# Attention's projections moved ahead of the delta rule's scan and the state space projections

## The chip, the core and the metric

The kernel runs on one core of a Trainium2 chip. The metric is device time in microseconds (us) of one execution; lower is better. The core has a matrix engine (PE, with its weight loads shown apart as PEld), a vector engine (DVE), a scalar engine (ACT), a general engine (POOL) and a queue (SP) that here issues most of the data transfers. Each engine runs its own instructions in a fixed order and waits where an input or a buffer is not ready.

## The reference

One layer of a hybrid encoder on x of 1024 tokens by 1024 channels, in float32. One normalised input feeds three mixers through one combined projection:

```python
h = rmsnorm(x, pre_mix_norm)
proj = h @ w_in        # columns: a_q, a_k, a_v | s_z, s_xbc, s_dt | g_qkv, g_z, g_b, g_a
att = swa_sink_alibi(a_q, a_k, a_v, sinks)      # 4 heads of 64, 2 key heads; keys of this and the 2 chunks before
ssd = ssd_mixer(s_z, s_xbc, s_dt, ...)          # causal conv of 4 taps, SiLU, chunked scan, gate, norm
gdn = gdn_mixer(g_qkv, g_z, g_b, g_a, ...)      # conv, SiLU, per chunk a triangular solve, then a scan
x = x + rmsnorm(concat[att, ssd, gdn] @ w_out, post_mix_norm)
h = rmsnorm(x, pre_ffn_norm)
x = x + rmsnorm((silu(h @ w_gate) * (h @ w_up)) @ w_down, post_ffn_norm)
```

Chunks are 64 tokens; the scans of ssd and gdn carry a state from chunk to chunk.

## The kernel before

**Two halves, then the feed-forward part.** Tokens are treated in two halves of 512, each in four tiles of 128 (t = 0 to 3). `half(h, hT, order)` runs the mixers of a half; `hT` is its normalised, transposed input, kept as a high and a low part so that each product is three matmuls (`gemm`, `gemm_rows`). Then comes the feed-forward block for all tokens, which the change does not touch.

**The steps of a half** are letters in a string of `ORD`, one string a half:

- K (`keys`): `decay_block` (the gate gz, decays), four convolved projections for keys and queries, for each tile `gdn_pre` (matmul `gram`, products `Wn`, `QK`), and at last `gdn_diag`: the diagonal blocks of all tiles are sent through memory (`cd`, `Wst`) and solved in 31 dependent steps on DVE, each a product `Tpr` and a sum `Tst`.
- V (`values`): two convolved projections gv.
- G0 to G3 (`scan`): with G0 and G2 the rest of the inverse (`gdn_inv`, matmuls lx, lv, lX, lV), then the scan of a tile.
- S0, S1 (`ssd_blocks`): per group four convolved projections (B, C, x0, x1) and the gate z. s00 to s13 (`ssd`): state space tile of group g and tile t; DVE scales the matrix `sE`, PE multiplies it in `y`.
- A (`att_blocks`): four projections without a convolution: two of queries (aq, whose weights are loaded as two halves of 64 columns), ak, av. a0 to a3 (`att`): two `att_tile` each, with PE's as, tp_p and ao.
- N (`after`): loads and normalises the next half's input into new `hT` tiles; they take the place of the old ones once the last projection of this half has read those.
- O (`block_first`, in the second half's string): the output projection, residual and norms of the first half; its `mT` also takes the place of `hT`.

**A convolved projection** (`conv_block`) is 24 matmuls, two splits of weights (high part on ACT, low part alternately on POOL and DVE), and on DVE three taps of 128x512 (line 348) and a last step (line 352); ACT copies, scales and takes a tanh. A gate projection (z) has 96 smaller matmuls, and per tile one tanh and one step of 128x256 on DVE (line 362). A projection of A has 24 matmuls, the splits, and one ACT copy.

**What sets the order.** The program is handed to a planner. The order of the text, and with it the order of the letters, is each instruction's priority; the planner fills every engine's queue with the first instruction by priority that by its own estimate is ready and has its buffer. Loads of weights have a raised priority. The order that comes out is fixed, and the engines keep to it. So a step that stands later in the string can still be placed earlier, as filler, where PE would otherwise stand still.

**Buffers that matter.** The pool tag "act" has `ACTS = 16` tiles of 128x512: a half takes 2 for gz, 2 for gv, 6 for each of S0 and S1 (B, C, x0, x1, two z), 4 for A; ak and av live on until a0 of the next half. Projections share two PSUM banks (`ps_mm`), raw weights three buffers, split weights six pairs.

The order of steps is read here:

```python
steps = dict(O=lambda: o0.append(block_first()), K=keys, V=values, G=scan, S=ssd_blocks, s=ssd, A=att_blocks, a=att, N=after)
for step in order.split():
    steps[step[0]](*[int(c) for c in step[1:]])
```

Of the kernel before, what the change touches and what calls it, by code (L numbers as in the profile page):

```python
# [28 lines left out]
KQS = 2  # L29
SB = 2  # L30
WC = 544
ORD = ("K V G0 G1 G2 G3 S0 s00 s01 s02 s03 S1 s10 s11 s12 s13 A N a0 a1 a2 a3",
       "K V G0 G1 G2 G3 S0 s00 s01 s02 s03 S1 s10 s11 s12 s13 A a0 a1 O a2 a3")
STEPS = (1, 1, 2)
EARLY = (2, 4)
LEAD, SLEAD = 260, 90
# [35 lines left out]
def trunk(ctx, tc, a):  # L72
# [855 lines left out]
    load_rest()  # L928
    hT = half(0, hT, ORD[0])
    half(1, hT, ORD[1])  # L930
    mT_h0 = o0[0]
# [388 lines left out]
```

## Time and profile before

| | |
|---|---|
| median of 3 runs | 1284.45 us (1283.5 to 1286.0) |
| profiled execution | 1280.08 us; span from first to last instruction 1278.3 us |
| PE busy | 1223.0 us, 96% of the span |
| DVE busy | 946.3 us, 74% |
| ACT busy | 574.6 us, 45% |
| POOL busy | 224.4 us, 18% |
| mean granted TensorE clock | 0.986 of full speed |
| data moved | 168.57 MB, mean 132 GB/s |

Busy time of an engine is the union of its instructions. "Idle before" an instruction is time its engine stood still just ahead of it, and the name behind the arrow is what released it. In a table by stretch the columns are busy us of each engine (or of the one chosen tile or line) with instruction counts in brackets, then the granted TensorE clock, the share of the transfer engines' time, and GB/s. L348 is line 348 of the kernel. The mixers of the first half lie at about 30 to 290 us, those of the second at about 235 to 550, overlapping.

### The profile page before, as it was taken

The numbers are of one execution on the slowest core, as the hardware profiler recorded it, in microseconds if no ns is written. First come the engines' busy times: TensorE is split into PE (matmuls) and PEld (weight loads), VectorE is DVE, ScalarE is ACT, GpSimd is POOL, SyncE is SP. The second block draws the span as 40 slices with busy tenths as digits, with TensorE's granted clock in tenths as the row PEclk, the third lists the DMA queues.
The fourth block names the chain that finished last, engine by engine and source line by source line (L and its number), as shares of the span: only waits on it lengthen the run. The fifth ranks groups of instructions, "written<-read, shape, count | busy, mean of one in ns | idle before, by whom it ended". The sixth has DMA issues, their size and how long they took to land.

```text
span 1278.3 us, 19099 instructions
## 1 busy us (share of the span) xinstructions
PE 1223.0 (96%) x6624; PEld 1017.1 (80%) x6624; DVE 946.3 (74%) x1890; ACT 574.6 (45%) x1261; POOL 224.4 (18%) x313
## 2 busy tenths in 40 slices
PE   5999999999998999978999999999999999999997
PEld 4878788887787889867987888888888887888885
DVE  5687996787799485653478998886676756768885
ACT  7454444455434353553456434333333334443661
POOL 3243455224344532100010000000000000000000
PEclk9999989999999999889999999999999999999999
DMA  7322332133332322366244465543333268676315
GB/s 238 83 72 78 87 82 74 48 104 91 97 79 57 94 96 67 108 211 219 92 162 165 148 221 164 168 142 97 124 102 113 97 231 287 185 229 214 94 57 197
DMA packets 161413, 168.57 MB, mean 132 GB/s; under 512 B 29567, under 2 KB 117915, under 8 KB 161317
## 3 DMA queue, kind: packets, MB, share of 16 engines
q1 hardware_dynamic: 143892, 133.53, 34.8%
q10 hardware_dynamic: 17424, 33.82, 7.0%
q8 instruction: 52, 0.85, 0.3%
q14 instruction: 45, 0.36, 0.1%
HBM read 127.21 MB, written 40.11 MB: 131 GB/s over the span
## 4 chain that ended last, share of the span: by engine, by line
PE 82%; DVE 9%; DMA 4%; ACT 2%; issue 1%; POOL 1%; SPq 0%; ACTq 0%; POOLq 0%; DVEq 0%
PE mm_p L1187 5%; PE mm_p L1188 5%; PE mm_p L1189 5%; PE mm_o L206 2%; PE mm_o L208 2%; PE mm_o L207 2%; DVE Tpr L513 1%; PE gram L487 1%; DMA yb<-in_ffn_w_down_dram 1%; PE y L676 1%; PE ao L755 1%; PE as L719 1%; PE mm_z L206 1%; PE mm_z L207 1%; PE mm_z L208 1%
## 5 line engine op out<-in xcount | busy, mean ns | idle before, releaser
L169 POOL TENSOR_TENSOR rsq<-ssv,mhalf 128x1 f32<-128x1 f32 x32 | 20.7, 655 | 752.2 <-DVE ssv L259 743.2
L513 DVE TENSOR_TENSOR Tpr<-Tst,Wst 128x32 f32<-128x32 f32 (+30 forms) x62 | 48.5, 782 | 4.4 <-POOL Wst L508 3.7
L206 PE MATMUL mm_o<-wh_wo,hhi_m 128*128 128x256 f32 x128 | 36.8, 287 | 1.1 <-DVE hlo_m L236 1.1
L206 PE MATMUL mm_z<-wh_z,hhi_a 128*128 128x256 f32 x128 | 37.7, 295 | 0.0
L208 PE MATMUL mm_z<-wh_z,hlo_a 128*128 128x256 f32 x128 | 36.6, 286 | 0.0
L207 PE MATMUL mm_z<-wl_z,hhi_a 128*128 128x256 f32 x128 | 36.5, 285 | 0.0
L208 PE MATMUL mm_o<-wh_wo,hlo_m 128*128 128x256 f32 x128 | 36.1, 282 | 0.0
L207 PE MATMUL mm_o<-wl_wo,hhi_m 128*128 128x256 f32 x128 | 36.0, 282 | 0.0
L676 PE MATMUL y<-xs,sE 128*128 128x64 f32 x128 | 19.9, 285 | 7.8 <-DVE sE L669 7.8
L1070 DVE TENSOR_TENSOR o<-mm_o,pm_row 128x256 f32<-128x256 f32 x16 | 6.8, 424 | 27.9 <-PE mm_o L208 27.9
L515 DVE TENSOR_REDUCE Tst<-Tpr 128x16 f32<-128x32 f32 (+30 forms) x62 | 26.7, 431 | 0.6
L676 PEld LDWEIGHTS y<-xs,sE 128*128 128x128 f32 x128 | 18.5, 203 | 9.7 <-DVE sE L669 8.4
L185 ACT ACTIVATE wh_wo<-wr_wo 128x512 fp32r<-128x512 f32 x24 | 15.1, 630 | 24.7 <-DMA es<-e00s 5.0
L206 PEld LDWEIGHTS mm_o<-wh_wo,hhi_m 128*128 128x128 f32 x128 | 24.1, 188 | 2.5 <-issue 1.9
L213 PE MATMUL mm_x<-hlo_a,wh_x 128*128 128x512 f32 x64 | 25.8, 403 | 0.0
L212 PE MATMUL mm_x<-hhi_a,wh_x 128*128 128x512 f32 x64 | 25.6, 400 | 0.0
L214 PE MATMUL mm_x<-hhi_a,wl_x 128*128 128x512 f32 x64 | 25.5, 398 | 0.0
L206 PEld LDWEIGHTS mm_z<-wh_z,hhi_a 128*128 128x128 f32 x128 | 24.8, 194 | 0.5
L207 PEld LDWEIGHTS mm_z<-wl_z,hhi_a 128*128 128x128 f32 x128 | 24.6, 192 | 0.3
L208 PEld LDWEIGHTS mm_z<-wh_z,hlo_a 128*128 128x128 f32 x128 | 24.7, 193 | 0.0
L208 PEld LDWEIGHTS mm_o<-wh_wo,hlo_m 128*128 128x128 f32 x128 | 24.1, 188 | 0.3 <-issue 0.3
L207 PEld LDWEIGHTS mm_o<-wl_wo,hhi_m 128*128 128x128 f32 x128 | 24.1, 188 | 0.0
(1683 smaller groups left out, 4481.4 us busy)
## 6 DMA issues: line engine op xcount, KB each, us to landing
wr_wo<-in_w_out_dram SPq DMA_DIRECT2D x32, 256.0 KB
x<-in_x_dram SPq DMA_DIRECT2D x8, 512.0 KB
wr_x<-in_w_in_dram SPq DMA_DIRECT2D x16, 256.0 KB
wr_z<-in_w_in_dram SPq DMA_DIRECT2D x16, 256.0 KB
res<-in_x_dram SPq DMA_DIRECT2D x8, 512.0 KB
resf<-x1d SPq DMA_DIRECT2D x8, 512.0 KB
mixn<-mixd SPq DMA_DIRECT2D x12, 256.0 KB
wr_e<-in_ffn_w_gate_dram SPq DMA_DIRECT2D x12, 256.0 KB
```

What stands on the lines that cost most here:

```text
L206: pe.matmul(ps, hi[:, tsl], whi, start=k == 0, stop=False)
L207: pe.matmul(ps, hi[:, tsl], wlo, start=False, stop=False)
L208: pe.matmul(ps, lo[:, tsl], whi, start=False, stop=k == len(wp) - 1)
L212: pe.matmul(ps, whi, hi, start=k == 0, stop=False)
L213: pe.matmul(ps, whi, lo, start=False, stop=False)
L214: pe.matmul(ps, wlo, hi, start=False, stop=k == len(wp) - 1)
L513: vec.tensor_tensor(pr[:, :, 0:i + 1], T[:, :, 0:i + 1], W[:, None, 0:i + 1, i].to_broadcast([P, CW, i + 1]), op=ALU.mult)
L515: vec.tensor_reduce(T[:, :, i], pr[:, :, 0:i + 1], axis=AX, op=ALU.add)
L676: pe.matmul(yd[:, j], E[:, j, :], xs[:, j], start=True, stop=True)
L1187: pe.matmul(ps[j], ah[:, s], bh, start=i == 0, stop=False)
L1188: pe.matmul(ps[j], ah[:, s], bl, start=False, stop=False)
L1189: pe.matmul(ps[j], al[:, s], bh, start=False, stop=i == NP - 1)
```

## The change

The letter A, four projections, moves in both strings from behind the last state space tile to the place right behind V. Nothing is added or removed; the instructions of A get a higher priority than those of G, S and s.

```diff
-ORD = ("K V G0 G1 G2 G3 S0 s00 s01 s02 s03 S1 s10 s11 s12 s13 A N a0 a1 a2 a3",
-       "K V G0 G1 G2 G3 S0 s00 s01 s02 s03 S1 s10 s11 s12 s13 A a0 a1 O a2 a3")
+ORD = ("K V A G0 G1 G2 G3 S0 s00 s01 s02 s03 S1 s10 s11 s12 s13 N a0 a1 a2 a3",
+       "K V A G0 G1 G2 G3 S0 s00 s01 s02 s03 S1 s10 s11 s12 s13 a0 a1 O a2 a3")
```

## The prediction

> **What bounds the kernel now.** I read the busy times by stage first, because the change moves work inside the first 640 us only. Columns: stretch, length, busy us of PE, PEld, DVE, ACT, POOL with instruction counts, granted TensorE clock, DMA share, GB/s.
>
> ```profile
> 64.00:115.00 51.00, 51.00 (x224) 37.10 (x223) 37.71 (x76) 27.41 (x59) 23.04 (x40) 1.00 0.31 84
> 115.00:187.00 72.00, 67.73 (x405) 59.02 (x404) 71.23 (x137) 29.23 (x71) 33.25 (x37) 0.95 0.27 72
> 347.00:416.00 69.00, 64.23 (x394) 56.15 (x393) 68.25 (x134) 31.74 (x76) 31.45 (x31) 0.98 0.27 71
> 528.00:576.00 48.00, 36.98 (x200) 31.51 (x200) 27.00 (x74) 25.19 (x65) 4.38 (x8) 0.82 0.60 189
> ```
>
> PE is the limit nearly everywhere. It falls short in one stretch of each half, where DVE is the limit (71.23 of 72 us, 68.25 of 69): PE idles 4.27 and 4.77 us there. The third hole is the end of the first half's output block, 11.02 us idle in 528 to 576. Total PE work does not change, so the result is what happens to these three holes.
>
> What fills DVE there is the delta rule's diagonal solve (the lines Tpr, Tst of gdn_diag): 31 dependent steps a half. First the timeline of DVE with the first and last step of each half, then the groups by line (busy us, mean ns, idle before).
>
> ```profile
> 115.05 0.20 DVE L513 TENSOR_TENSOR Tpr<-Tst,Wst 128x32 f32<-128x32 f32 x1 [2.48 <-POOL Wst L508]
> 186.61 0.67 DVE L515 TENSOR_REDUCE Tst<-Tpr 128x16 f32<-128x512 f32 x1
> 344.98 1.27 DVE L513 TENSOR_TENSOR Tpr<-Tst,Wst 128x32 f32<-128x32 f32 x1 [1.23 <-POOL Wst L508]
> 414.50 0.68 DVE L515 TENSOR_REDUCE Tst<-Tpr 128x16 f32<-128x512 f32 x1
> ...
> L513 DVE TENSOR_TENSOR Tpr<-Tst,Wst 128x32 f32<-128x32 f32 (+30 forms) x62 | 48.5, 782 | 4.4 <-POOL Wst L508 3.7
> L515 DVE TENSOR_REDUCE Tst<-Tpr 128x16 f32<-128x32 f32 (+30 forms) x62 | 26.7, 431 | 0.6
> ```
>
> So (48.5 + 26.7) / 2 = 37.6 us of a 72 us stretch are the solve, and the convolved projections and state space tiles beside it take the rest. The PE timeline and the list of PE's waits show how that reaches PE, which runs in its written order: it stands at a state space tile's matmul until DVE has scaled sE.
>
> ```profile
> 162.49 0.69 PE L676 MATMUL y<-xs,sE 128*128 128x64 f32 x2 [3.96 <-DVE sE L669]
> 396.03 0.74 PE L676 MATMUL y<-xs,sE 128*128 128x64 f32 x4 [3.60 <-DVE sE L669]
> ...
> PE y L676 <- DVE sE L669: 7.8, 3, 4.0
> PE tp_f L230 <- ACT o L878: 5.5, 2, 3.7
> ```
>
> **The change, part by part.** *Moved matmuls.* A is four projections of 24 matmuls a half. One costs 47.50 - 41.94 = 5.56 us, by the first matmuls of two neighbours in the PE timeline; four make 22.2 us. In before they run, interleaved, from 179.13 to 214.98, right after the solve.
>
> ```profile
> 41.94 0.40 PE L212 MATMUL mm_gk<-hhi_a,wh_gk 128*128 128x512 f32 x1
> 47.50 0.40 PE L212 MATMUL mm_gq<-hhi_a,wh_gq 128*128 128x512 f32 x1
> ...
> 179.13 0.58 PE L212 MATMUL mm_aq<-hhi_a,wh_aq 128*128 128x512 f32 x1
> 214.98 0.40 PE L214 MATMUL mm_av<-hhi_a,wl_av 128*128 128x512 f32 x1
> ```
>
> Where they go is seen from the stretch 80 to 115 by tile: S0's B, then its two x.
>
> ```profile
> 80.00:115.00 35.00, 6.49 (x24) 1.00 0.32 88
> 80.00:115.00 35.00, 11.60 (x48) 1.00 0.32 88
> ```
>
> V has ended by 80, and S0's four convolved blocks (B, C at 6.5 each, x 11.6: 24.6) fill the stretch with 35 - 24.6 = 10.4 us of other matmuls, mostly K's small ones. With A in their place it is 80 + 22.2 + 10.4, so A ends near 113, about where the solve begins. PE was full there and stays full: cost 0 by itself. The same holds for half 1, where the solve's first step is 230 us later.
>
> *What stands beside the solve.* Pushed back by 22 us, S0's four convolved blocks now start near 113 instead of 80. PE's share of the stretch by tile, first z, then aq, then x, B, C (the last three add up to 24.8 in the stretch):
>
> ```profile
> 115.00:187.00 72.00, 25.62 (x191) 0.95 0.27 72
> 115.00:187.00 72.00, 6.88 (x27) 0.95 0.27 72
> 115.00:187.00 72.00, 12.18 (x48) 0.95 0.27 72
> 115.00:187.00 72.00, 6.34 (x24) 0.95 0.27 72
> 115.00:187.00 72.00, 6.26 (x24) 0.95 0.27 72
> ```
>
> z is light for DVE, a convolved block heavy. DVE's share, first the three taps (L348), then the last step (L352), then the group means of the z gate and of aq's split:
>
> ```profile
> 115.00:187.00 72.00, 13.76 (x15) 0.95 0.27 72
> 115.00:187.00 72.00, 4.08 (x6) 0.95 0.27 72
> ...
> L362 DVE SCALAR_TENSOR_TENSOR z<-gth_z,mm_z 128x256 f32<-128x256 f32 x16 | 6.6, 410 | 0.0
> L186 DVE TENSOR_TENSOR wl_aq<-wr_aq,wh_aq 128x512 fp32r<-128x512 f32 x4 | 4.3, 1081 | 0.0
> ```
>
> Out of the stretch go the second z (half of 25.62 = 12.8 us of PE), aq (6.9) and both x of S1 (12.2), 31.9 in all. In come S0's four blocks (24.8 by the same rows) and, to fill up, the first x of S1 (6.1): PE -1.0. DVE goes from five blocks (15 taps) to seven: +2 x (13.76 + 4.08) / 5 = +7.1; four z gates fewer, -4 x 0.41 = -1.6; two aq splits fewer, -2 x 1.08 = -2.2. DVE +3.3. Where DVE sets the length, PE's idle grows by 3.3 + 1.0 = 4.3 us a half.
>
> *The head start.* Before 115, DVE gets A's splits (the cheapest split row is 0.69; four, 2.8) in place of about three blocks (3 x 3.57 = 10.7): 7.9 us of DVE are free while gdn_pre makes the solve's input. If all of that shortened the road to the solve, it would start 7.9 us earlier beside light work; if PE's order sets that road, 0. The row says DVE already waited there for ACT, and DVE idled 51 - 37.71 = 13.3 us of that stretch, so I take nearer the low end, 2.3 us. Net +2.0 a half, **+4.0** for both; bounds -3.6 x 2 and +4.3 x 2.
>
> ```profile
> 99.87 0.69 DVE L471 TENSOR_REDUCE ssq<-sq 128x8 f32<-128x512 f32 x1 [1.94 <-ACT sq L466]
> ```
>
> *Buffers.* The pool "act" has 16 tiles. In before gz 2, gv 2, S0 6 and S1 6 fill it exactly, and A waits until S0's are free. Now A holds 4 until the last attention tile, and S1 finds two; its other x and z wait until S0's tiles are through, as A did. In half 1 the previous ak and av hold two more until a0. Their matmuls can run ahead into the two ps_mm banks; behind the evacuation that waits on ACT stand the next splits. Between nothing (today's wait for the same release hides) and a stall of one tile's round a half (the larger gap above, 3.96, twice, = 8), I take 0, since state space and attention tiles are ready for PE meanwhile.
>
> *DMA queue.* aq's weights come as halves. A issues 12 loads a half, against 8 for four convolved projections, so 4 more stand on SP in front of S0's loads and of the solve's own stores and loads.
>
> ```profile
> 147.42 12.42 SPq L184 DMA_DIRECT2D wr_aq<-in_w_in_dram  x8
> ...
> L184 SPq DMA_DIRECT2D wr_aq<-in_w_in_dram x16: 368/432/1009, 147.4 to 392.6; - x16
> ```
>
> 4 x 0.43 = 1.7 us of issue. The loads are covered by the three raw buffers and a full PE; without that cover, or if the solve's loads are what comes late, it is 1.7 us of later solve a half. I take 0 of 0 to 1.7.
>
> *The tiles a0 to a3* become ready 100 us earlier and are the planner's filler for PE's gaps. What is spent there is missing later: in 528 to 552 their tiles as, tp_p and ao keep PE busy beside the normalisation chain of O.
>
> ```profile
> 528.00:552.00 24.00, 3.20 (x8) 0.79 0.33 108
> 528.00:552.00 24.00, 2.83 (x12) 0.79 0.33 108
> 528.00:552.00 24.00, 4.07 (x24) 0.79 0.33 108
> ...
> L726 DVE SCALAR_TENSOR_TENSOR asc<-cst,as 128x256 f32<-128x256 f32 (+1 forms) x32 | 11.6, 398 | 6.7 <-PE as L719 6.7
> L729 DVE TENSOR_REDUCE am<-asc 128x2 f32<-128x512 f32 (+1 forms) x16 | 10.4, 648 | 0.2
> ```
>
> PE 10.1 us for about three of the 16 attention tiles, 3.4 each; DVE 22.0 / 16 = 1.4 each in these two rows alone, with six smaller operations behind, so as filler beside the solve they bring no large gain. Done before 528, they leave up to 10.1 us more idle (+10.1); left where they are, 0. a2 and a3 still stand behind O, so I take **+1.5**, about half a tile.
>
> *Clock.* The stretches after the 3.96 us gap show what a gap costs beyond itself: 8 x 0.31 + 8 x 0.12 = 3.4 us of clock at most. I count no new gap, 0 of 0 to 3.4 a half.
>
> ```profile
> 158.00:166.00 8.00, 4.04 (x19) 3.67 (x18) 8.00 (x14) 2.30 (x4) 3.65 (x5) 0.69 0.28 68
> 166.00:174.00 8.00, 8.00 (x58) 7.50 (x57) 8.00 (x17) 2.75 (x9) 2.93 (x3) 0.88 0.12 33
> ```
>
> The Trainium skill, "TensorE: Matmul & The Clock Gate", section "What's actually happening", says that an idle window of about 3.4 us halves the array's clock until it was busy about as long; the trace agrees (gap 3.96 us, clock 0.69 then 0.88). By it, 4.3 us added as one new gap in each half would cost an estimated 1.7 us more each, and the sum would be +8.9 in place of +5.5.
>
> **Sum:** +4.0 + 1.5 = +5.5 us. The profiled execution took 1280.08 us (span 1278.3), 4.4 below the median of the three runs, 1284.45; on that median I get **1290**.
>
> **Rivals.** *Faster, by the head start:* if the solve starts 4.3 us earlier than today (before 111 and 341 us), the stretch breaks even; from there on each us closes the holes, at most 4.27 + 4.77, so 1284.45 - 9 = 1275.4. For it: 13.3 us of idle DVE ahead of the solve. Against: PE's dense order sets where gdn_pre's gram matmuls come. *Faster, at the end:* attention's rows of half 1 are stored earlier, the second output block's transposes move up and fill the 11.02 us hole; with most of it, -8, 1276. Against: that hole's own chain waits for o (5.5 us on ACT alone), and the loads share a queue. *No change:* filler replaces filler, holes trade places, 1284.5. For it: PE's total is the same and 96% busy. *Clearly slower, by buffers:* S1 stalls for S0's tiles in both halves, 8 us, on top of the +5.5: 1298. *The change does nothing,* because the planner issues by readiness: part of no change, unlikely since A is ready as soon as V is.
>
> **How the numbers follow.** 0.2% is 2.6 us, about what a measurement of this kernel can tell from no change. Chances: forecast 0.33 (1287.1 to 1294), buffers 0.12, no change 0.23, head start 0.20, end 0.12. So slower 0.45, same 0.23, faster 0.32. Range: the fast cases reach to 1275.4, the buffer case to 1298 with 3.4 of clock on top; leaving out a tenth at each end gives 1277 to 1301; the forecast's own is 1287 to 1294.
>
> **What the profile after would show.** Right: aq's matmuls near 80 and 310 us; the solve starting 2 us earlier and taking longer; PE's waits for sE above 7.8 us; S1's second z after the solve; fewer attention matmuls after 528 us. Wrong: PE idle under 4 us in both stretches, or the solve ending before 180 us; or the hole after 528 filled by tp_m.

## The result, and the profile after

The changed kernel takes 1300.77 us, the median of four runs (1297.55 to 1305.57), against 1284.03 (1283.5 to 1286.0) for the kernel before in the same session. The ratio is 1.0131, with a 95% interval of 1.009 to 1.0171: slower by 16.7 us. The forecast was 1290 with a range to 1301, so the sign is right and the measured change is three times the forecast one.

The profiled execution took 1297.55 us (span 1295.7, mean granted clock 0.973; before 1278.3 and 0.986). PE's busy time rose from 1223.0 to 1235.0 us and its idle time from 55.3 to 60.7. The work is the same, so the 12 us more of busy time are the same matmuls at a lower clock: clock withheld over the span is (1 - 0.973) x 1295.7 = 35.0 us against (1 - 0.986) x 1278.3 = 17.9. The feed-forward part is not touched: its first matmul (e00p) comes at 580.3 us, before at 562.1, and the whole 17.4 us of longer span are there by then.

By stretch, after (the columns are those of the prediction's first fence):

```profile
115.00:187.00 72.00, 67.97 (x371) 56.19 (x369) 67.55 (x132) 31.33 (x71) 29.27 (x40) 1.00 0.31 83
187.00:234.00 47.00, 45.31 (x459) 41.52 (x459) 36.63 (x90) 21.54 (x56) 22.26 (x34) 0.93 0.20 52
347.00:416.00 69.00, 66.21 (x343) 53.73 (x342) 56.04 (x124) 30.31 (x70) 25.92 (x32) 0.98 0.29 81
416.00:464.00 48.00, 40.41 (x308) 35.33 (x308) 34.43 (x69) 16.64 (x42) 19.17 (x30) 0.79 0.14 39
```

In the two stretches that the prediction read as the solve's, PE idles 4.03 us (4.27 before) and 2.79 us (4.77 before). In the second half this compares different work: the solve now begins at 366.8 us and ends at 432.6, so it reaches into the next stretch, and DVE is busy only 56.04 of 69 us in 347 to 416 because the solve is not there at first. Cut at the solve's own first and last step, before and then after, the second half reads:

```profile
344.98:415.18 70.20, 65.43 (x398) 56.92 (x397) 69.58 (x135) 31.13 (x75) 31.85 (x31) 0.98 0.26 68
366.83:432.61 65.78, 57.77 (x298) 47.06 (x297) 64.50 (x133) 24.48 (x60) 23.47 (x25) 0.90 0.23 65
```

PE idles 8.01 us beside the second half's solve, 4.77 before; beside the first half's it is 3.85 against 4.26. By stretch, the loss shows behind the two that the prediction read, in 187 to 234 and above all in 416 to 464. The kernel before had there:

```profile
187.00:234.00 47.00, 46.35 (x364) 39.08 (x364) 32.69 (x89) 23.76 (x68) 23.33 (x39) 1.00 0.28 70
416.00:464.00 48.00, 47.41 (x367) 39.81 (x365) 29.54 (x80) 22.77 (x60) 21.88 (x35) 1.00 0.23 70
```

In 416 to 464 PE's idle time grew from 0.59 to 7.59 us and the clock fell from 1.00 to 0.79; in 187 to 234 idle grew from 0.65 to 1.69 and the clock fell to 0.93. Together that is 8.0 us of idle and 13.4 us of withheld clock (0.21 x 48 + 0.07 x 47), which overlap where PE stood still at a low clock. Over the whole of 416 to 464 no engine is full. In its first part one is: from 412 to 428 us DVE is busy 15.65 of 16 us (the slices below), with the end of the solve and the steps of the state space scan, while PE is busy 8.5. So two things have to be explained: what PE waits for there, and why it has no other work meanwhile, as it had before.

ACT's timeline shows why there is no other work. A convolved projection is taken out of PSUM by two ACT steps: a small copy (L342, `cb_`), and the scaled copy (L346) that writes an act tile. Before, in the second half's S1, they are 0.48 us apart:

```profile
377.43 0.58 ACT L342 ACTIVATE cb_C<-mm_C 128x512 f32<-128x512 f32 x1
377.91 0.77 ACT L346 ACTIVATE C<-mm_C,wconv 128x512 f32<-128x512 f32 x1
```

After, for S1's C and its x tiles:

```profile
409.35 0.58 ACT L342 ACTIVATE cb_C<-mm_C 128x512 f32<-128x512 f32 x1
412.90 0.58 ACT L342 ACTIVATE cb_x<-mm_x 128x512 f32<-128x512 f32 x1
426.29 0.78 ACT L346 ACTIVATE C<-mm_C,wconv 128x512 f32<-128x512 f32 x1
436.24 0.58 ACT L342 ACTIVATE cb_x<-mm_x 128x512 f32<-128x512 f32 x1
440.63 1.45 ACT L346 ACTIVATE x<-mm_x,wconv 128x512 f32<-128x512 f32 x2
```

C waits 426.29 - 409.35 = 16.9 us, the first x 440.63 - 412.90 = 27.7. Until then both ps_mm banks are held, and no projection can fill PE's gaps. In PE's timeline of the same time, only the state space scan of S0 is left, and each of its own waits is bare:

```profile
412.39 0.60 PE L744 MATMUL tp_p<-cst,asc 128*128 128x128 f32 x4
415.29 1.21 PE L676 MATMUL y<-xs,sE 128*128 128x64 f32 x8 [2.30 <-DVE sE L669]
...
422.27 0.79 PE L441 MATMUL D_s<-mask_r,ident_r 128*128 128x512 f32 x1 [4.14 <-DVE ssd_st L690]
...
426.44 0.69 PE L676 MATMUL y<-xs,sE 128*128 128x64 f32 x2 [1.08 <-DVE sE L669]
427.12 0.79 PE L212 MATMUL mm_x<-hhi_a,wh_x 128*128 128x512 f32 x1
```

What PE waits for is DVE, which does the scan's steps in between those of the solve. The sum `sz` is complete at 418.1, and DVE, busy all the time, adds it to `ssd_st` at 421.80:

```profile
418.06 0.89 DVE L513 TENSOR_TENSOR Tpr<-Tst,Wst 128x432 f32<-128x432 f32 x1
...
421.27 0.61 DVE L515 TENSOR_REDUCE Tst<-Tpr 128x16 f32<-128x448 f32 x1
421.80 0.41 DVE L690 TENSOR_TENSOR ssd_st<-ssd_st,sz 128x256 f32<-128x256 f32 x1
```

What lets C go is seen in the timeline of all engines, here DVE and ACT just before 426.29:

```profile
423.88 0.42 DVE L692 TENSOR_TENSOR y<-y,z 128x256 f32<-128x256 f32 x1
...
424.14 1.15 ACT L449 ACTIVATE sE<-D_s,ncs 128x128 f32<-128x128 f32 x4 [10.66 <-PE D_s L445]
...
425.89 0.42 ACT L694 ACTIVATE xw<-y 128x256 f32<-128x256 f32 x1
```

DVE's product at 423.88 is the last use of the first z tile of S0 (it holds the gate of tiles 0 and 1; the state space tile whose matmuls ran at 415 to 418 is the second of S0's four). ACT, whose order has C's L346 behind the work of that scan, stood 10.66 us waiting for the scan's D_s, and took C out after it. (The profile does not number the buffers; which tile C takes is inferred from the program and these times.) The next x goes on at 427.12, in the bank that C has left. The waiting x is taken out at 440.63, just behind the transposes of S0's fourth tile (438.48 to 439.25). That is a circle: S1's projections wait for S0's tiles, S0's tiles for S0's scan, and the scan's waits for a full DVE have no projections to lie beside. The low clock, in slices of 4 us:

```profile
412.00:416.00 4.00, 1.70 (x13) 1.33 (x11) 3.97 (x8) 1.12 (x2) 2.27 (x3) 1.00 0.40 125
416.00:420.00 4.00, 2.12 (x8) 1.26 (x7) 3.86 (x7) 0.00 (x0) 0.61 (x1) 0.57 0.10 34
420.00:424.00 4.00, 1.73 (x5) 1.21 (x5) 4.00 (x9) 0.00 (x0) 0.73 (x1) 0.50 0.20 66
424.00:428.00 4.00, 2.92 (x10) 2.32 (x10) 3.82 (x9) 2.76 (x9) 1.88 (x3) 0.50 0.00 0
440.00:444.00 4.00, 3.34 (x40) 3.28 (x41) 1.55 (x3) 2.85 (x7) 2.61 (x5) 0.56 0.24 70
```

### The profile page after: what moved, and what is told of

Same layout as the page of the kernel before. It is cut to its first block, busy times and chain, and to the rows that moved or that the text cites. A ratio compares the mean times of both kernels' runs of the same rounds, so it can differ in the third digit from the quotient of the medians.

```text
span 1295.7 us, 19103 instructions
## 1 busy us (share of the span) xinstructions
PE 1235.0 (95%) x6624; PEld 1029.0 (79%) x6624; DVE 947.3 (73%) x1890; ACT 575.9 (44%) x1261; POOL 221.0 (17%) x313
## 4 chain that ended last, share of the span: by engine, by line
PE 79%; DVE 11%; DMA 5%; issue 2%; ACT 2%; POOL 1%; SPq 0%; ACTq 0%; POOLq 0%; DVEq 0%
PE mm_p L1187 5%; PE mm_p L1189 5%; PE mm_p L1188 5%; DVE Tpr L513 2%; PE mm_o L206 2%; PE mm_o L208 2%; PE mm_o L207 2%; DVE Tst L515 1%; DMA yb<-in_ffn_w_down_dram 1%; PE gram L487 1%; PE as L719 1%; PE ao L755 1%; PE mm_z L206 1%; PE mm_gz L206 1%; PE mm_z L207 1%
## 5 line engine op out<-in xcount | busy, mean ns | idle before, releaser
L449 ACT ACTIVATE sE<-D_s,ncs 128x128 f32<-128x128 f32 x64 | 18.3, 370 | 23.6 <-PE D_s L445 23.5
L735 ACT ACTIVATE asc<-asc,anm 128x256 f32<-128x256 f32 (+1 forms) x32 | 15.7, 490 | 26.7 <-DVE anm L731 23.5
L206 PE MATMUL mm_gz<-wh_gz,hhi_a 128*128 128x272 f32 x64 | 22.8, 357 | 0.4 <-DVE hlo_a L236 0.4
```

The source lines that it names most:

```text
L206: pe.matmul(ps, hi[:, tsl], whi, start=k == 0, stop=False)
```

## The experiments

The theory after the result: the changed order lacks act tiles; A holds four from the time of V on, and S1 is left with two. Rivals: the heavier neighbours of the solve on DVE (the term +4.0 of the forecast) by themselves, and the later solve and attention of the second half by themselves. Times are medians, ratios are to the kernel before on the same chip.

**e1_half0 and e2_half1: the new string in one half only.**

```diff
 e1_half0: ORD[0] = "K V A G0 G1 G2 G3 S0 ... s13 N a0 a1 a2 a3"    ORD[1] as before
 e2_half1: ORD[0] as before    ORD[1] = "K V A G0 G1 G2 G3 S0 ... s13 a0 a1 O a2 a3"
```

> A moved ahead in the first half only, the second half as before. Theory late attention (half 0's attention tiles run at 259 to 330 us in place of 215 to 294 and hold gdn_pre of half 1 back, so that half 1's solve starts 22 us late): this string alone carries it, solve of half 1 starts after 360 us, time 1292 to 1298. Theory buffers (S1's outputs wait for S0's 16-tile pool, worst in half 1 where the previous ak and av are still held): half 1 is free of it, time within 3 us of before, 1281 to 1287, solve of half 1 starts near 345.

> A moved ahead in the second half only. Theory buffers: the hole of about 10 us behind 410 us with the low clock is there, time 1292 to 1298. Theory late attention: half 0 is as before, the solve of half 1 starts near 345 us, no new hole, time 1283 to 1288.

e1_half0: 1284.38 us, ratio 1.0009 (0.9994 to 1.0024), no change. The last sum of the second half's solve starts at 431.0 there, nearly as late as in the changed kernel (431.9) and 16.5 us later than before. So a late solve with late attention costs nothing by itself. Its first half has the changed kernel's waits too, an x from 188.30 to 205.26 (17.0 us), and the clock of 187 to 234 is 1.00 there: a drift of the two steps alone need not cost anything.

e2_half1: 1292.01, 1.0066 (1.0041 to 1.009), half of the loss. There S1's C waited from 407.45 to 421.33 and an x from 410.39 to 438.60, but the solve had ended at 407.0, and PE idled 2.68 us beside it. The hole of 10 us that the buffers theory expected is not there: in 412 to 464 PE idles 3.5 us (0.6 before), and 6.7 us of clock are withheld in 416 to 464. The fall of the clock stands beside waits of less than 1 us each; four slices of 4 us:

```profile
412.00:416.00 4.00, 2.01 (x55) 1.76 (x55) 1.77 (x4) 0.75 (x2) 3.18 (x7) 1.00 0.43 132
416.00:420.00 4.00, 3.49 (x48) 3.25 (x44) 1.92 (x5) 0.00 (x0) 0.90 (x2) 0.51 0.16 26
420.00:424.00 4.00, 4.00 (x20) 3.14 (x19) 2.42 (x5) 3.46 (x10) 2.79 (x6) 0.50 0.06 11
424.00:428.00 4.00, 4.00 (x19) 3.34 (x18) 2.88 (x8) 1.20 (x2) 2.23 (x6) 0.50 0.09 33
```

The two halves by themselves (0.0009 and 0.0066) do not add up to 0.0131. PE's idle time beside the second half's solve fits this: 4.77 us before, 4.67 in e1_half0 (late solve, no wait for tiles in that half), 2.68 in e2_half1 (wait for tiles, but behind the solve), 8.01 where both meet. These are four single profiled executions, and no run separates the two any further.

**e3_acts20 and e4_ws4: more act tiles, and the control.** Four tiles more need room, so both have four pairs of split weights in place of six.

```diff
 e3_acts20: ACTS = 16 -> 20, WS = 6 -> 4, changed order
 e4_ws4:    ACTS = 16,       WS = 6 -> 4, changed order
```

> The changed kernel with 20 in place of 16 tiles in the pool act, paid for with 4 in place of 6 pairs of split weights. To be read against the changed kernel with 4 pairs. Theory buffers: S1 no longer waits for S0's tiles, at least 8 us faster than that control, no wait of 2 us or more on PE between 400 and 430 us. Theory late attention or DVE beside the solve: within 4 us of the control.

> Control: the changed kernel with 4 in place of 6 pairs of split weights and 16 tiles in act. All theories: 0 to 8 us slower than the changed kernel, 1298 to 1309, with the hole behind 410 us still there.

e3_acts20: 1286.08, 1.0018 (1.0002 to 1.0035). e4_ws4: 1297.54, 1.0099 (1.0076 to 1.0122). Four tiles are worth 11.5 us, all else equal. PE idles 4.59 us beside the second half's solve in e3_acts20 and 8.07 in e4_ws4, with the same order and so the same neighbours. (e4_ws4 came out 0.5 us under its expected range, and one wait of PE in e3_acts20, 2.10 us for a weight split on POOL, is just above the 2 us that were to be its limit.) ACT's pair for S1's C and PE's stretch, e3_acts20:

```profile
407.42 0.58 ACT L342 ACTIVATE cb_C<-mm_C 128x512 f32<-128x512 f32 x1
407.90 0.77 ACT L346 ACTIVATE C<-mm_C,wconv 128x512 f32<-128x512 f32 x1
```

```profile
416.00:464.00 48.00, 43.70 (x387) 39.80 (x387) 37.33 (x85) 24.07 (x62) 22.86 (x35) 0.93 0.33 107
```

The same pair in e4_ws4, and from its list of PE's waits one that names the held bank (a projection's matmul waits for ACT to take C out):

```profile
411.58 0.58 ACT L342 ACTIVATE cb_C<-mm_C 128x512 f32<-128x512 f32 x1
419.87 0.76 ACT L346 ACTIVATE C<-mm_C,wconv 128x512 f32<-128x512 f32 x1
```

```profile
PE mm_x L212 <- ACT C L346: 2.1, 1, 2.1
```

**e5_before12 and e6_before20: the old order with fewer and with more tiles.**

```diff
 e5_before12: ACTS = 16 -> 12, WS = 6, old order
 e6_before20: ACTS = 16 -> 20, WS = 6 -> 4, old order
```

> The old order with 12 in place of 16 tiles in act, so that S1 finds two tiles until S0's are free, as in the changed kernel. Theory buffers: the old order gets the same illness, S1's scaled copies on ACT (line 346) come 10 us or more after their plain copies (line 342), 1292 to 1305. Theory order (what hurts is A's work ahead of the solve, not the tiles): 1282 to 1288.

> The old order with 20 tiles in act and 4 pairs of split weights. Theory buffers: A no longer waits for S0's tiles, 1276 to 1283, and the changed order with the same tiles (1286.1) is 3 us or more slower than this. If the order is worth something of itself once the tiles are there, this is at or above 1286.

e5_before12: 1302.97, 1.015 (1.0116 to 1.0184). Four tiles taken from the old order make the same picture as A's four held early, C waiting 23.6 us:

```profile
381.70 0.58 ACT L342 ACTIVATE cb_C<-mm_C 128x512 f32<-128x512 f32 x1
392.74 0.78 ACT L346 ACTIVATE B<-mm_B,wconv 128x512 f32<-128x512 f32 x1
405.29 0.80 ACT L346 ACTIVATE C<-mm_C,wconv 128x512 f32<-128x512 f32 x1
```

e6_before20 gave 1288.99, 1.0037 (1.002 to 1.0055), against an expectation that had it no slower than before: a miss. Part of the price is in the feed-forward part. From e00p to the end the kernel before takes 716.2 us, e6_before20 721.7, e3_acts20 720.2, e4_ws4 719.9: two pairs of split weights fewer cost some 4 to 5 us there. In the mixers' part e6_before20's profiled execution is late too (e00p at 568.8, before at 562.1); it was 3.2 us above the median of its kernel and the one of the kernel before 4.0 us below, so how much of this is the kernel stays open. e3_acts20 stands 0.0018, 2.3 us, above the kernel before, less than the price of its split weights. At or above 1286 the expectation's other branch holds, that the order is worth something once the tiles are there. But the changed order with 20 tiles is ahead by only 0.0019, and the two intervals overlap.

**e7_after_G and e8_mid20: A at other places.**

```diff
 e7_after_G: "K V G0 G1 G2 G3 A S0 ...", both halves, 16 tiles, WS = 6
 e8_mid20:   "K V G0 ... S0 s00 s01 s02 s03 A S1 ...", both halves, 20 tiles, WS = 4
```

> The changed kernel with A behind G0 to G3 and still ahead of S0, in both halves. G cannot start before the solve ends, so its place against A should not matter: both theories 1296 to 1306, as the changed kernel. If being ahead of the scan is what hurts, 1284 to 1290.

> A between the tiles s00 to s03 and S1, 20 tiles in act, 4 pairs of split weights: A's matmuls, light for DVE, lie beside the solve. Theory DVE beside the solve (the prediction's term of 4 us): faster than the changed order with the same tiles by 4 us or more, 1276 to 1282. Theory buffers: as that, within 3 us, 1283 to 1289.

e7_after_G: 1298.26, 1.0119 (1.0064 to 1.0173). Behind the scan or ahead of it makes no difference that these runs could tell; ahead of S0 does, with C again waiting 17.2 us:

```profile
405.25 0.57 ACT L342 ACTIVATE cb_C<-mm_C 128x512 f32<-128x512 f32 x1
422.44 0.78 ACT L346 ACTIVATE C<-mm_C,wconv 128x512 f32<-128x512 f32 x1
```

e8_mid20 was to be faster if heavy neighbours of the solve cost time, since S0 then stands beside it no more than before and A lies between. It took 1296.67, 1.0102 (1.0075 to 1.0129), 10.6 us more than e3_acts20 with the same buffers. Its pairs are 0.5 us apart; e00p comes at 571.7 (e3_acts20: 567.2), and the feed-forward part takes 722.7. So both theories missed: the buffers theory had it within 3 us of e3_acts20. Nor does the run refute the rival about DVE. With A's light matmuls beside the solve PE did idle less there, 2.12 and 2.56 us in the two halves against 3.00 and 4.59 in e3_acts20; the time went elsewhere. Why this place of A is worse, beside the larger hole at the end of the first half's output block, was not followed up:

```profile
528.00:576.00 48.00, 34.41 (x196) 30.32 (x195) 26.40 (x75) 24.16 (x65) 6.19 (x10) 0.75 0.49 152
```

**e9_after20 and e10_before20: 20 tiles without the price.** The two missing pairs of split weights are given back for the feed-forward part, in a pool of their own that is opened behind the first half's output block.

```diff
-        return [wsp.tile([P, WC], F32R, tag=tg, ...) for tg in ("wh", "wl")]
+        turn2[0] += phase[0] == 2
+        pool_ = wsp2[0] if phase[0] == 2 and turn2[0] % 3 == 0 else wsp
+        return [pool_.tile([P, WC], F32R, tag=tg, ...) for tg in ("wh", "wl")]
```

> Changed order, 20 act tiles, with four pairs of weight splits until the first half's output block and two more pairs (every third load from them) behind it, where the space of the first part is free again. Buffers theory: the changed order lost by its act tiles alone, and the 2 us that e3_acts20 stayed above the kernel before are the weight splits missing in the feed-forward part (that part took 720.2 us against 716.2). Given back, 1281 to 1284, ratio 0.997 to 1.000: no slower than before. If the order itself costs something beside the buffers (heavier neighbours of the solve, fewer attention tiles as filler), 1286 or more, as e3_acts20.

> The old order with the same pools as e9_after20. Buffers theory: it had tiles enough with 16, so 20 bring it nothing: 1283 to 1286, ratio 0.999 to 1.002, and the changed order is level with it or up to 3 us ahead. If 20 tiles help any order by themselves, 1277 to 1281, and then e9_after20 says nothing of the order.

e9_after20: 1283.35 (11 runs), ratio 1.0007 (0.9995 to 1.002). e10_before20: 1284.71 (11 runs), 1.001 (1.0001 to 1.0019). From e00p to the end they take 714.9 and 715.7 us. With tiles enough, the changed order is level with the kernel before; the two orders cannot be told apart, as each one's interval holds the other's ratio. The stretch where the changed kernel lost, in e9_after20 and then in e10_before20:

```profile
416.00:464.00 48.00, 43.44 (x389) 40.05 (x388) 36.32 (x86) 20.79 (x52) 23.64 (x39) 0.93 0.31 100
```

```profile
416.00:464.00 48.00, 47.79 (x368) 40.16 (x367) 29.35 (x84) 21.43 (x60) 21.95 (x37) 1.00 0.25 69
```

The 4.6 us of idle time that the changed order still has there are mostly the solve's own, at another place: its solve ends at 424.6, that of e10_before20 at 414.5, and in 347 to 416 it is the other way round, 1.10 us idle against 4.05. Beside the second half's whole solve PE idles 4.84 us in e9_after20 and 4.05 in e10_before20, with 8.01 in the changed kernel. So heavy neighbours alone are worth little; the loss needs the missing tiles.

**e11_attS1 and e12_attS0: let the tiles go earlier instead.** 16 tiles and six pairs as in the changed kernel, but the attention tiles moved forward in both halves.

```diff
 e11_attS1: "K V A G0 G1 G2 G3 S0 s00 s01 s02 s03 a0 a1 a2 a3 S1 s10 ... s13 N" (second half: O in place of N)
 e12_attS0: "K V A a0 a1 a2 a3 G0 G1 G2 G3 S0 ... s13 N" (second half: O in place of N)
```

> The changed order, 16 act tiles, 6 pairs of weight splits, with one thing moved: the attention tiles a0 to a3 stand ahead of S1 (behind s03) in both halves, so that A's four tiles and the two of the half before are let go earlier. Buffers theory: S1's C and x find tiles soon after their matmuls (the evacuation by ACT, L346, follows the copy L342 within 3 us, against 17 and 28 us in the changed kernel), and no wait of PE above 2.5 us stands in 347 to 464: 1284 to 1290. Theory that the early place of A costs by what stands beside the solve: still 1295 to 1301, since the solve has the same neighbours. If the attention tiles take DVE from the solve, the gap moves there and the time is 1290 to 1296.

> The changed order, 16 act tiles, 6 pairs of weight splits, with the attention tiles a0 to a3 directly behind A in both halves, ahead of G and S0. In e11_attS1, with them behind s03, the attention tiles did not run earlier than the solve's end and S1's evacuations waited as before (C copied at 427.28, evacuated at 438.03). Here they have nothing of the scan in front of them. Buffers theory: if their matmuls (as) of half 1 run before 400 us, the six tiles of A and of the half before are free when S1 comes, the evacuation L346 follows the copy L342 within 3 us, no wait of PE above 2.5 us stands in 347 to 464, and the time is 1284 to 1290. If the attention tiles' steps on DVE push the solve back instead, the pairs are close together too, but the solve of half 1 ends after 436 us (432.6 in the changed kernel) and the time is 1290 to 1298. If the pairs are close together and the time is still 1298 or more with no later solve, act tiles are not what the changed kernel lost by.

e11_attS1: 1309.56, 1.0191 (1.0173 to 1.0208), the slowest kernel here and outside what all three theories gave. Its place in the string did not bring attention forward: in the second half 24 of its 40 as matmuls start at 456.1 us or later, behind the solve, and by then S1 had been waiting:

```profile
427.28 0.58 ACT L342 ACTIVATE cb_C<-mm_C 128x512 f32<-128x512 f32 x1
438.03 0.78 ACT L346 ACTIVATE C<-mm_C,wconv 128x512 f32<-128x512 f32 x1
```

So the wait was not removed, and the run does not test the price of it. e12_attS0: 1298.88, 1.0111 (1.0088 to 1.0134). Here attention did run earlier, though not before 400 us as the expectation asked: its last as matmul of the second half stands at 434.5. S1's C found its tile:

```profile
425.21 0.57 ACT L342 ACTIVATE cb_C<-mm_C 128x512 f32<-128x512 f32 x1
425.69 0.76 ACT L346 ACTIVATE C<-mm_C,wconv 128x512 f32<-128x512 f32 x1
```

```profile
416.00:464.00 48.00, 48.00 (x381) 41.25 (x380) 34.68 (x83) 22.15 (x54) 15.73 (x24) 1.00 0.21 58
540.00:588.00 48.00, 31.45 (x183) 28.25 (x182) 24.69 (x61) 23.20 (x59) 6.36 (x11) 0.75 0.55 179
```

The hole in 416 to 464 is gone altogether, 48.00 of 48 us busy at full clock, with no later solve (its last sum starts at 419.5). Taken by its letter, the expectation's last sentence now says that act tiles were not the cause, because the time stayed at 1298.88. That sentence assumed that nothing else would get worse, and two things did. In the first half an x still waited 6.4 us (188.23 to 194.64; clock 0.88 in 187 to 234). And attention was spent: the hole at the end of the output block, 11.02 us of idle in the kernel before and 11.77 in the changed one (540 to 588), is 16.55 us at clock 0.75. This is the "missing as filler" that the forecast bounded with 10.1 us. At e00p the two kernels are level (579.6 here, 580.3 in the changed one), but no run puts the two prices apart. The runs e3_acts20 and e4_ws4, which differ in the tiles alone, carry the conclusion; e12_attS0 shows that the same hole closes by another way, and that the time is then lost elsewhere.

## Why the prediction was right in sign and wrong in size

The sign came by another way than forecast. The +5.5 us were to come from the neighbours of the solve (+4.0) and from missing attention (+1.5), and neither did by itself. The loss came from two terms that the sum took as 0, buffers and clock. That 1300.77 still lies in the range, 0.23 us from its end, is owed to the rival "by buffers", which set that end.

*Moved matmuls* (0): right. A's first matmul stands at 83.7 us, S0's first convolved block at 118.5 (forecast 80 and near 113), and PE is busy all 51 us of 64 to 115.

*What stands beside the solve* (+4.3 a half before the head start, +4.0 in the sum): this step failed. The heavy neighbours did come, and more of them than forecast: PE's matmuls of B, C and x in 115 to 187 rose from 24.8 to 46.9 us (11.61, 11.79 and 23.47 by tile), DVE's taps there from 13.76 to 16.27. But the solve became shorter (61.0 us in place of 72.2 in the first half, 65.8 in place of 70.2 in the second), and PE's idle time beside it fell from 4.26 to 3.85 us in the first half. In the second it rose from 4.77 to 8.01, but with the same neighbours and 20 tiles it is 4.59 and 4.84 (e3_acts20, e9_after20). The solve's sums in the two halves, after:

```profile
L515 DVE TENSOR_REDUCE Tst<-Tpr x31: 189/425/683, 116.8 to 175.8; 128x16 f32<-128x32 f32 x1, 128x16 f32<-128x48 f32 x1, 128x16 f32<-128x64 f32 x1, 128x16 f32<-128x80 f32 x1
L515 DVE TENSOR_REDUCE Tst<-Tpr x31: 190/425/690, 367.1 to 431.9; 128x16 f32<-128x32 f32 x1, 128x16 f32<-128x48 f32 x1, 128x16 f32<-128x64 f32 x1, 128x16 f32<-128x80 f32 x1
```

The first half's solve ended at 176.5, 10.8 us earlier than before, which the forecast had named as a sign against it ("the solve ending before 180"). The waits for sE, which it wanted above 7.8 us, fell to 3.4; with the 4.1 us for ssd_st, a step of the same scan on DVE, it is 7.5. The step took a full DVE for a DVE that sets PE's length. Convolved matmuls run ahead of their taps (in 115 to 187 the matmuls of eight blocks, but the taps of six), and as long as PE had them it had work beside the solve. Where they ran out, from 412 us on, the full DVE did set PE's pace.

*Head start* (2.3): in the first half the solve starts at 115.6, 0.5 later than before, but K itself was 2.8 us late (first tp_kq at 67.9 instead of 65.1), so the head start within the half was there at the forecast size. e9_after20 against e10_before20 shows it again: from the first tp_kq to the solve it is 47.6 us in place of 49.9. In the second half the solve starts at 366.8, 21.9 us later: attention tiles of the first half and projections are placed ahead of it. e1_half0 shows that this alone costs nothing.

*Attention missing as filler* (+1.5): not so in the changed kernel. From 540 to 588, the place of the old hole, PE idles 11.77 us against 11.02. Where attention is spent in full that hole is larger, 16.55 us in e12_attS0.

*DMA queue* (0 of 0 to 1.7 a half): not seen. Between 60 and 440 us PE waits for no transfer, and ACT's waits there for raw weights fell from 14.6 to 5.4 us.

*Buffers* (taken as 0 of 0 to 8) is the term of the sum that was mis-sized. The forecast's upper bound of 8 us of idle is what came: 7.00 more in 416 to 464 and 1.04 more in 187 to 234. The reason given for 0, that state space and attention tiles are ready for PE meanwhile, failed at both ends. The state space tiles at hand are S0's, the very ones whose scan is waited for, on a DVE that is full; and of attention in the second half nothing was placed there, its as matmuls stand at 364 to 389 and then from 499 on:

```profile
L719 PE MATMUL as<-ak,aq x24: 376/376/480, 499.2 to 552.8; 64*128 64x256 f32 x24
L724 PE MATMUL as<-ak,aq x8: 272/272/374, 364.6 to 388.9; 64*128 64x128 f32 x8
```

*Clock* (taken as 0 of 0 to 3.4 a half) was mis-sized too: 10.1 us are withheld in 416 to 464 and 3.3 in 187 to 234. The second figure is not explained by the waits for tiles, since e1_half0 has the same ones there at a clock of 1.00. The Trainium skill, "TensorE: Matmul & The Clock Gate", section "What's actually happening", ties the lower clock to an idle window of about 3.4 us. The trace agrees in part: PE has a longer gap, 4.14 us up to 422.27, and the clock is 0.50 in it and behind it. But the clock fell earlier, behind a gap of 2.30 us: in slices of 1 us it is 0.78 in 416 to 417 and 0.50 from there on, and the long gap began at 418.1. The slices at 440 to 444 (0.56, waits of 0.95 and 1.41 us) and those of e2_half1 show a fall without such a gap as well; there the measurement decides.

*The rivals.* "Clearly slower, by buffers" (1298, with 3.4 us of clock on top 1301) had the right mechanism, at a chance of 0.12, and its 8 us of idle time were met. Its number is partly luck: it holds the +5.5 us, which did not come, in place of most of the 13.4 us of clock, which did. A solve that starts 4.3 us earlier and a filled end did not happen, and "no change" is what remains when the tiles are there (e9_after20). The share that stays open: the first tp_kq came 2.8 us later in the changed kernel with the clock at 0.89 instead of 0.97 in the first 64 us, though the instructions up to there stand in the same order. It came at 64.3 to 65.4 in some kernels here and at 66.2 to 68.4 in others, of both orders, so it is not an effect of A's place alone; its cause was not found.

## What to carry to other kernels

A step moved forward takes its buffers with it: count, for each pool, what is held at the place the step moves to and until when, and ask what the next step in line will find. Where the pool runs out, the bound is not the one wait that the release causes but every wait that the blocked work used to cover, with the clock on top; a filler that itself needs the held tiles to be released is no filler. The sign in the timeline is two steps of one eviction that drift apart while their engine stands idle. Whether it costs anything depends on what else is there: beside a full DVE it did, in the first half of e1_half0 it did not. And when a change moves a stage, cut the stretches anew at the stage's own first and last step before comparing them.

## What the runs showed of the hardware

The granted clock does not only fall behind long gaps. In e2_half1 it was 0.51, 0.50 and 0.50 in three slices in which PE was recorded busy 3.49, 4.00 and 4.00 of 4 us, behind a slice in which it was busy 2.01 of 4, idle in waits below 1 us; what stands there are matmuls of 32x32, 64x64 and 24x128 among the others. In the changed kernel it was 0.50 from 226 to 232 us although PE is recorded busy without a gap from 214 on. Whether the small size of the matmuls or something else lowers the clock was not tried by itself. So a loss of 10 us in one stretch can be mostly clock, and PE's busy share alone (1235.0 us, more than before) hides it.
